# One 256-column step for the scores of the first 128 queries in the attention of a decoder block, its halves added by VectorE ahead of the sigmoid

## The chip, the cores and the metric

One core of a Trainium2 chip runs the whole program once. The metric is the device time in microseconds (us) of one execution, with the median of a few runs as the kernel's time. A profiled execution gives, beside its time, the span from its first to its last instruction and a record of each instruction on each engine.

## The reference, cut to what matters

One decoder layer on 512 tokens of width 1024, in float32: a norm, one input projection, two token mixers side by side (a chunkwise matrix memory with 8 heads, and stick-breaking attention with 8 heads), gates, an output projection, a norm, and a squared-ReLU MLP. The change lies in the scores of the attention:

```
def stick_breaking(q, k, v):
    ...
    for blk in range(S // QBLK):                       # QBLK = 128 queries
        t0, t1 = blk * QBLK, (blk + 1) * QBLK
        z = jnp.einsum('bqhd,bshd->bhqs', q[:, t0:t1], k[:, :t1]) * scale
        ...
        log_keep = jnp.where(strict, jax.nn.log_sigmoid(-z), 0.0)
        suffix = lax.cumsum(log_keep, axis=3, reverse=True) - log_keep
        A = jnp.where(strict, jnp.exp(jax.nn.log_sigmoid(z) + suffix), 0.0)
        outs.append(jnp.einsum('bhqs,bshd->bqhd', A, v[:, :t1]))
```

So query block 0 (the first 128 queries) sees 128 keys, block 1 sees 256, block 2 384 and block 3 512. The other mixer matters only because its second half of heads is worked on right after the first four attention heads: its queries and keys (`q_a`, `k_a`) go through a causal convolution of four taps and a SiLU first.

## The kernel before, in words

**Two parts per number.** Most products are made from float32 values split in two: a high part in the matmul's format (a cast on ScalarE, ACT) and the rest (value minus high part, on VectorE, DVE). `mm3` then issues three matmuls on TensorE (PE): high by high, high by low, low by high, all added up in PSUM. A weight block of 256 rows by 512 columns is loaded by `stage` into `raw_...`, split into `whi_...` (L114, ACT) and `wlo_...` (L115, DVE), and there are four buffers for each of the two, so that the fifth block's cast waits until PE has used the first. PSUM has eight banks of 512 columns: four for projections (`pp_...`), four for everything else.

**Order.** `ORDER` lists the steps by hand: `... s0 T1 s1 oa0 s2 s3 qka1 ga0 r4 r5 va1 m4 r6 m5 r7 qkb2 ...`. The steps are written out in that order, and a scheduler in the compiler then sets the order of the instructions on each engine, from that order, from stated priorities and from its own estimates of when each is ready. An engine works through its list in that fixed order. A change of one step can so move rows of other steps.

**Attention head** (`s0` to `s7`, function `sb_head`): `SEG` lists the four query blocks by j, block 3-j with n keys at column o of the head's 1280 columns of scores: j=0 has 512 columns, j=1 384, j=3 128 and j=2 256. The scores stand in three banks, `zb{h}_0` (j=0), `zb{h}_1` (j=1 and, behind it, j=3) and `zb{h}_2` (j=2, 256 columns; the other 256 are not used). For each block and each sign ACT makes a sigmoid from PSUM into `r` (of -z) and `b` (of z), L557. GpSimd (POOL) sets the upper part of each diagonal block of `b` to zero (L560), DVE makes the running products of `r` (L565) and multiplies them into `b` (L566). PE then transposes `b` in ten pieces into `zt` (L571), ACT and DVE split that into `ah` and `al` (L575, L576), and PE multiplies with the values into `po` (`mm3`).

**What comes next to heads 2 and 3.** The step `qka1` takes the projected q and k of the second four heads of the matrix memory (`xc10` to `xc13`): four taps on DVE into `cy10` to `cy13` (L399, then three rounds of L402), a sigmoid on ACT back into `xc` (L404), their product (L406), then the split into `qh1`, `ql1` and `kk1` (ACT L415 and L419, DVE L416, L418 and L420). `ga0` is a gate projection (`pp_ga`, the sigmoids `g_ga` on ACT L600, a multiply on DVE L605), `va1` the projection of the values (`pp_va`, split into `va1` by L180 and L181). `decay` for heads 4 to 6 makes exponentials `rb` on ACT (L442). Step `m4` is head 4 of the matrix memory: its scores `za4` (L451, L453), DVE scales them (L458), ACT and DVE split them into `ph4` (L460) and `pl4`, and PE multiplies them with the values into `pn4`. `qkb2` is the next projection (`pp_qkb`).

Of the kernel before, what the change touches and what calls it, by code (L numbers as in the profile page):

```python
# [10 lines left out]
AF = mybir.ActivationFunctionType  # L11
# [5 lines left out]
P = 128  # L17
# [8 lines left out]
SEG = ((0, 0, 512), (1, 512, 384), (3, 896, 128), (2, 1024, 256))  # L26
OFF = {j: o for j, o, _ in SEG}
# [5 lines left out]
HT = 256  # L33
# [30 lines left out]
def block_kernel(ctx: ExitStack, tc: tile.TileContext, x, norm_mix_g, w_in, b_if, b_gate, conv_w, mlstm_norm_g,  # L64
                 sb_q_norm_g, sb_k_norm_g, w_out, norm_mlp_g, w_up, w_down, out):
    nc = tc.nc
    act, dve, pool, pe = nc.scalar, nc.vector, nc.gpsimd, nc.tensor
# [10 lines left out]
    def f5(name):  # L78
        return ah_.tile([P, LIN], F32, tag="f5", name=name, bufs=3)

    def bank(name):
        return ps_a.tile([P, S], F32, tag="pa", name=name)

    def half_square(name):

        b = [bank(f"{name}{i}") for i in range(3)]
        return [(b[0], 0, 512), (b[1], 512, 512), (b[2], 1024, 256)]

    def part(banks, o, n):
        b, c, _ = banks[o // S]  # L90
        return b[:, o - c:o - c + n]

    def r5(name):
        return ah_.tile([P, LIN], F32R, tag="r5", name=name, bufs=4)

    def t2(tag, bufs, name):
        return at.tile([P, S], F32, tag=tag, name=name, bufs=bufs)
# [20 lines left out]
    def mm3(o, ah, al, bh, bl, start, stop, **kw):  # L118
        pe.matmul(o, ah, bh, start=start, stop=False, **kw)  # L119
        pe.matmul(o, ah, bl, start=False, stop=False, **kw)  # L120
        pe.matmul(o, al, bh, start=False, stop=stop, **kw)  # L121
# [425 lines left out]
    def sb_head(h, q, k, rq, v):  # L547

        z = half_square(f"zb{h}_")
        for j, o, n in SEG:  # L550
            il = slice((3 - j) * P, (4 - j) * P)
            mm3(part(z, o, n), q[:, 0, il], q[:, 1, il], k[:, 0, :n], k[:, 1, :n], j != 3, True,
                skip_group_check=True)
        b, r = f5(f"b{h}"), f5(f"r{h}")
        for j, o, n in SEG:
            for w, d in ((1, r), (0, b)):
                act.activation(d[:, o:o + n], part(z, o, n), AF.Sigmoid, scale=rq[:, w, 3 - j, h % 2:h % 2 + 1])  # L557
        for j, o, n in SEG:
            d = slice(o + n - P, o + n)
            pool.affine_select(out=b[:, d], in_=b[:, d], pattern=[[-1, P]], compare_op=ALU.is_gt, fill=0.0, base=0,  # L560
                               channel_multiplier=1)

        for j, o, n in SEG:
            kr = r[:, o:o + n][:, ::-1]
            dve.tensor_tensor_scan(kr, kr, msk[:, S - n:][:, ::-1], 1.0, ALU.mult, ALU.max)  # L565
        dve.tensor_mul(b[:, :LIN - 1], b[:, :LIN - 1], r[:, 1:LIN])  # L566
        zt = half_square(f"zt{h}_")
        for j, o, n in SEG:
            for i in range(j, 4):
                oi = OFF[3 - i] + P * j  # L570
                pe.transpose(part(zt, o + P * (i - j), P), b[:, oi:oi + P], ident)  # L571
        ah, al = r5(f"ah{h}"), r5(f"al{h}")
        for zz, c, n in zt:
            e = slice(c, c + n)
            act.copy(ah[:, e], zz[:, :n])  # L575
            dve.tensor_sub(al[:, e], zz[:, :n], ah[:, e].bitcast(F32))  # L576
        po = bank(f"po{h}")
        c = slice((h % 4) * P, (h % 4 + 1) * P)
        for j, o, n in sorted(SEG):
            mm3(po[:, j * P:], v[j][:, 0, c], v[j][:, 1, c], ah[:, o:o + n], al[:, o:o + n], j == 0, j == 3,  # L580
                skip_group_check=True)
        yb = t2("sy", 8, f"yb{h}")
        act.copy(yb, po)
        return yb
# [74 lines left out]
    def step(n):  # L659
        kind, i = n[:-1], int(n[-1])  # L660
        if n == "qkb1":
            load_pool[:] = [(wp, "raw", 2), (at, "raw", 1), (wp, "raw", 2)]
        if kind == "qka":
            got[n] = qka(i)
        elif kind == "r":
            got[n] = decay(i, got["qka1"][3] if i > 3 else got["qka0"][4])
        elif kind == "m":
            got[n] = mlstm_head(i, got[f"qka{i // 4}"], (v0, v1)[i // 4], got[f"r{i}"])
        elif kind == "n":
            mlstm_norm(i, [got[f"m{h}"] for h in range(i, i + 4)])  # L670
        elif kind == "va":
            v_chunk("va1", C_VA + 512, v1)
        elif kind == "vb":
            v_chunk(n, C_VB + 512 * i, vb[i])
        elif kind == "qkb":
            got[n] = qkb(i)
        elif kind == "T":
            got[n] = pair_T(got[f"qkb{i}"], i)
        elif kind == "s":
            yb[i] = sb_head(i, *got[f"T{i // 2}"][i % 2], vb[i // 4])  # L680
        elif kind == "oa":
            a_gate(i, "oa", C_OA, None)
        elif kind == "ga":
            a_gate(i, "ga", C_GA, 8)
        else:
            b_gate_(i, yb[4 * i:4 * i + 4])
# [286 lines left out]
```

## Time and profile before

| | us |
|---|---|
| time, median of 3 runs | 819.48 |
| lowest and highest of the 3 | 818.83, 820.11 |
| the profiled execution's own time | 818.37 |
| its span | 816.6 |

The profiled execution lies 1.1 us (0.14%) under the median, and 1.8 us of its time lie around its span. TensorE's granted clock was 1.00 throughout. A row of the timeline reads: start, duration, engine, line, operation, output<-inputs, sizes, count, and in brackets the idle time before it and who ended that. A matmul's end is modelled and matmuls overlap, so the spacing of their starts says what one costs. "PEld" are the loads of the stationary operand, which overlap matmuls.

### The profile page before, as it was taken

How to read it: one execution, taken by the hardware profiler on the slowest of the kernel's cores; microseconds unless marked ns; L12 is line 12 of the kernel's file. 1: busy time of each engine (PE TensorE's matmuls, PEld its weight loads, DVE VectorE, ACT ScalarE, POOL GpSimd, SP SyncE). 2: the span in 40 equal slices, each digit the busy share in tenths (PEclk: the TensorE clock that was granted, in tenths of full speed). 3: DMA queues.
4: the chain of work that ended last, by engine and by line, in shares of the span. 5: the costliest groups of instructions: out<-in, count | busy, mean ns of one | idle time of the engine just before them, and what ended most of it. 6: DMA issues, size and time to landing. Idle time of an engine off the chain costs nothing.

```text
span 816.6 us, 11540 instructions
## 1 busy us (share of the span) xinstructions
PE 806.2 (99%) x4380; PEld 692.7 (85%) x4380; DVE 599.1 (73%) x826; ACT 457.3 (56%) x681; POOL 165.0 (20%) x216
## 2 busy tenths in 40 slices
PE   8999999999999999999999999999999999999998
PEld 6878887888888887888888888999999999999876
DVE  6669967584598486756653659898689868978994
ACT  6429756654557468545552437576466545655541
POOL 3015323111221140010120101223302421232220
PEclk9999999999999999999999999999999999999999
DMA  9354542353423423522257406987977995999963
GB/s 233 91 156 143 120 80 64 82 104 84 152 91 94 118 65 67 142 66 77 78 188 270 109 4 155 208 178 160 204 226 158 182 224 166 188 200 188 228 125 100
DMA packets 64408, 113.65 MB, mean 139 GB/s; under 512 B 5793, under 2 KB 18129, under 8 KB 64354
## 3 DMA queue, kind: packets, MB, share of 16 engines
q1 hardware_dynamic: 44770, 71.43, 31.3%
q0 software_dynamic: 19584, 41.50, 26.6%
q8 instruction: 34, 0.56, 0.3%
q14 instruction: 20, 0.16, 0.1%
HBM read 110.74 MB, written 2.17 MB: 138 GB/s over the span
## 4 chain that ended last, share of the span: by engine, by line
PE 93%; DVE 3%; ACT 1%; DMA 1%; issue 1%; SPq 0%; ACTq 0%; DVEq 0%
PE pp_qkb L121 4%; PE pp_qkb L119 4%; PE pp_qkb L120 4%; PE pp_yup L119 3%; PE pp_yup L120 3%; PE pp_yup L121 3%; PE ydn L119 2%; PE ydn L120 2%; PE ydn L121 2%; PE pp_qka L119 2%; PE pp_zup L120 2%; PE pp_va L120 2%; PE pp_zup L121 2%; PE pp_qka L120 2%; PE pp_xup L120 2%; PE pp_zup L119 2%
## 5 line engine op out<-in xcount | busy, mean ns | idle before, releaser
L560 POOL TENSOR_SCALAR_AFFINE_SELECT b<-b 128x128 f32<-128x128 f32 x32 | 19.0, 609 | 161.3 <-ACT b L557 161.3
L120 PE MATMUL pp_qkb<-wlo_qkb,hT 128*128 128x512 f32 x128 | 50.2, 392 | 0.0
L121 PE MATMUL pp_qkb<-whi_qkb,hT 128*128 128x512 f32 x128 | 50.0, 393 | 0.0
L119 PE MATMUL pp_qkb<-whi_qkb,hT 128*128 128x512 f32 x128 | 49.3, 391 | 0.0
L766 POOL DMA_DIRECT2D raw_Xup<-in_w_up_dram x24 | 28.9, 1243 | 84.8 <-DVE wlo_p5up L727 37.6
L766 POOL DMA_DIRECT2D raw_Xdn<-in_w_down_dram x18 | 21.6, 1214 | 102.6 <-DVE wlo_p5dn L727 36.1
L565 DVE TENSOR_TENSOR_SCAN r<-r,msk 128x512 f32<-128x512 f32 (+3 forms) x32 | 25.1, 832 | 13.8 <-ACT r L557 13.8
L115 DVE TENSOR_TENSOR wlo_qkb<-raw_qkb,whi_qkb 128x1024 fp32r<-128x1024 f32 x16 | 21.7, 1365 | 14.1 <-ACT whi_qkb L114 14.0
L119 PEld LDWEIGHTS pp_qkb<-whi_qkb,hT 128*128 128x128 f32 x128 | 24.1, 188 | 5.1
L121 PEld LDWEIGHTS pp_qkb<-whi_qkb,hT 128*128 128x128 f32 x128 | 24.0, 188 | 5.1
L120 PEld LDWEIGHTS pp_qkb<-wlo_qkb,hT 128*128 128x128 f32 x128 | 24.1, 188 | 4.7
L897 ACT ACTIVATE uq<-uq 128x512 f32<-128x512 f32 x32 | 20.0, 630 | 12.2 <-DVE uq L896 12.0
L120 PE MATMUL pp_va<-wlo_va,hT 128*128 128x512 f32 x64 | 24.9, 392 | 0.8 <-DVE wlo_va L292 0.8
L119 PE MATMUL pp_ga<-hT,whi_ga 128*128 128x512 f32 x64 | 25.3, 395 | 0.0
L119 PE MATMUL pp_qka<-hT,whi_qka 128*128 128x512 f32 x64 | 25.2, 396 | 0.0
L120 PE MATMUL pp_qka<-hT,whi_qka 128*128 128x512 f32 x64 | 25.2, 393 | 0.0
L121 PE MATMUL pp_oa<-hT,wlo_oa 128*128 128x512 f32 x64 | 25.1, 392 | 0.0
L120 PE MATMUL pp_wo<-wlo_wo,y 128*128 128x512 f32 x64 | 25.1, 392 | 0.0
L120 PE MATMUL pp_ga<-hT,whi_ga 128*128 128x512 f32 x64 | 25.1, 392 | 0.0
L120 PE MATMUL pp_oa<-hT,whi_oa 128*128 128x512 f32 x64 | 25.1, 392 | 0.0
L119 PE MATMUL pp_vb<-whi_vb,hT 128*128 128x512 f32 x64 | 25.0, 391 | 0.0
L120 PE MATMUL pp_gb<-hT,whi_gb 128*128 128x512 f32 x64 | 25.0, 391 | 0.0
(571 smaller groups left out, 2955.2 us busy)
## 6 DMA issues: line engine op xcount, KB each, us to landing
raw_Xup<-in_w_up_dram POOLq DMA_DIRECT2D x24, 512.0 KB, 7.2
raw_Xdn<-in_w_down_dram POOLq DMA_DIRECT2D x18, 512.0 KB, 6.9
raw_qkb<-in_w_in_dram SPq DMA_DIRECT2D x32, 256.0 KB, 3.9
rb<-rows POOLq DMA_DIRECT2D x8, 640.0 KB, 5.4
raw_va<-in_w_in_dram SPq DMA_DIRECT2D x8, 512.0 KB, 5.2
raw_qka<-in_w_in_dram SPq DMA_DIRECT2D x16, 256.0 KB, 6.6
raw_vb<-in_w_in_dram SPq DMA_DIRECT2D x8, 512.0 KB, 4.5
raw_oa<-in_w_in_dram SPq DMA_DIRECT2D x8, 512.0 KB, 4.2
```

The source lines that it names most:

```text
L115: dve.tensor_sub(lo, raw, hi.bitcast(F32))
L119: pe.matmul(o, ah, bh, start=start, stop=False, **kw)
L120: pe.matmul(o, ah, bl, start=False, stop=False, **kw)
L121: pe.matmul(o, al, bh, start=False, stop=stop, **kw)
L560: pool.affine_select(out=b[:, d], in_=b[:, d], pattern=[[-1, P]], compare_op=ALU.is_gt, fill=0.0, base=0, channel_multiplier=1)
L565: dve.tensor_tensor_scan(kr, kr, msk[:, S - n:][:, ::-1], 1.0, ALU.mult, ALU.max)
L766: pool.dma_start(out=buf[b, j], in_=src(more, j), accum_op=ALU.add)
L897: act.activation(h(r, c), h(r, c), AF.Square)
```

## The change

Per head, the three matmuls of query block 0 (128 columns each) go. In their place, behind the three of j=2, stand one matmul of 256 columns (L555: the high part of the queries by both parts of the keys, into the unused half of `zb{h}_2`) and one of 128 columns (L556: the low part of the queries by the high part of the keys, added to the first half). ACT then copies the first half into `b` (L558), DVE adds the second half to it (L559), and the two sigmoids of j=3 read `b` in place of PSUM.

```diff
-        for j, o, n in SEG:
+        for j, o, n in sorted(SEG)[:3]:
             il = slice((3 - j) * P, (4 - j) * P)
-            mm3(part(z, o, n), q[:, 0, il], q[:, 1, il], k[:, 0, :n], k[:, 1, :n], j != 3, True,
-                skip_group_check=True)
+            mm3(part(z, o, n), q[:, 0, il], q[:, 1, il], k[:, 0, :n], k[:, 1, :n], True, True, skip_group_check=True)
+
+        x = z[2][0][:, HT:].rearrange("p (w n) -> p w n", w=2)
+        pe.matmul(x, q[:, 0, :P], k[:, :, :P], start=False, stop=False, skip_group_check=True)
+        pe.matmul(x[:, 0, :], q[:, 1, :P], k[:, 0, :P], start=False, stop=True, skip_group_check=True)
         b, r = f5(f"b{h}"), f5(f"r{h}")
+        act.copy(b[:, OFF[3]:OFF[3] + P], x[:, 0, :])
+        dve.tensor_add(b[:, OFF[3]:OFF[3] + P], x[:, 1, :], b[:, OFF[3]:OFF[3] + P])
         for j, o, n in SEG:
             for w, d in ((1, r), (0, b)):
-                act.activation(d[:, o:o + n], part(z, o, n), AF.Sigmoid, scale=rq[:, w, 3 - j, h % 2:h % 2 + 1])
+                act.activation(d[:, o:o + n], part(z, o, n) if j != 3 else b[:, o:o + n], AF.Sigmoid,
+                               scale=rq[:, w, 3 - j, h % 2:h % 2 + 1])
```

Lines behind the edit have numbers that are six higher than before (the sigmoid L557 is L562, the transposes L571 are L577). The scheduler's order moves as well, most of all between head 1 and head 5 of the attention.

Place 1, PE, the scores of head 2; before:

```order
L119 MATMUL zb2_1_1775<-kT2_1549,qT2_1541 128x384
L120 MATMUL zb2_1_1775<-kT2_1549,qT2_1541 128x384
L121 MATMUL zb2_1_1775<-kT2_1549,qT2_1541 128x384
L119 MATMUL zb2_1_1775<-kT2_1549,qT2_1541 128x128
L120 MATMUL zb2_1_1775<-kT2_1549,qT2_1541 128x128
L121 MATMUL zb2_1_1775<-kT2_1549,qT2_1541 128x128
L119 MATMUL zb2_2_1776<-kT2_1549,qT2_1541 128x256
L120 MATMUL zb2_2_1776<-kT2_1549,qT2_1541 128x256
L121 MATMUL zb2_2_1776<-kT2_1549,qT2_1541 128x256
```

and with the change:

```order
L119 MATMUL zb2_1_1777<-kT2_1550,qT2_1542 128x384
L120 MATMUL zb2_1_1777<-kT2_1550,qT2_1542 128x384
L121 MATMUL zb2_1_1777<-kT2_1550,qT2_1542 128x384
L119 MATMUL zb2_2_1778<-kT2_1550,qT2_1542 128x256
L120 MATMUL zb2_2_1778<-kT2_1550,qT2_1542 128x256
L121 MATMUL zb2_2_1778<-kT2_1550,qT2_1542 128x256
L555 MATMUL zb2_2_1778<-kT2_1550,qT2_1542 128x256
L556 MATMUL zb2_2_1778<-kT2_1550,qT2_1542 128x128
```

Three matmuls of 128 columns became one of 256 and one of 128, behind j=2.

Place 2, PE, from the last projection matmul of `va1` to the scores of head 4 of the matrix memory and on; before:

```order
L121 MATMUL pp_va13_2283<-whi_va13_2376,hT1_151 128x512
L451 MATMUL za4_0_2416<-qh10_2078,kk10_2079 128x512
L453 MATMUL za4_0_2416<-ql10_2080,kk10_2079 128x512
...
L451 MATMUL za4_2_2418<-qh10_2078,kk10_2079 128x256
L453 MATMUL za4_2_2418<-ql10_2080,kk10_2079 128x256
L119 MATMUL pp_qkb20_2530<-whi_qkb20_2537,hT0_150 128x512
L120 MATMUL pp_qkb20_2530<-wlo_qkb20_2538,hT0_150 128x512
L121 MATMUL pp_qkb20_2530<-whi_qkb20_2537,hT1_151 128x512
```

and with the change:

```order
L121 MATMUL pp_va13_2287<-whi_va13_2380,hT1_151 128x512
L451 MATMUL za4_0_2420<-qh10_2082,kk10_2083 128x512
L453 MATMUL za4_0_2420<-ql10_2084,kk10_2083 128x512
...
L451 MATMUL za4_2_2422<-qh10_2082,kk10_2083 128x256
L453 MATMUL za4_2_2422<-ql10_2084,kk10_2083 128x256
L119 MATMUL pn4_2445<-ph4_2431,va10_2408 128x512
L451 MATMUL za5_0_2477<-qh10_2082,kk10_2083 128x512
```

Before, 27 matmuls of the projection `qkb2` stand between `za4` and the first of `pn4`; now `pn4`, which reads `ph4`, follows `za4` at once, and `qkb2` comes after it and after `za5`.

Place 3, DVE and ACT, around the convolution of `qka1`, behind attention head 3. DVE before:

```order
L576 TENSOR_TENSOR al3_1892<-zt3_0_1878,ah3_1891 128x512
L576 TENSOR_TENSOR al3_1892<-zt3_1_1879,ah3_1891 128x512
L576 TENSOR_TENSOR al3_1892<-zt3_2_1880,ah3_1891 128x256
L115 TENSOR_TENSOR wlo_va11_2317<-raw_va11_2314,whi_va11_2316 128x1024
L399 TENSOR_SCALAR cy10_2050<-xc10_2042,vec_128 128x512
```

and with the change (`g_ga00` to `g_ga02` are gates of `ga0`):

```order
L582 TENSOR_TENSOR al3_1896<-zt3_2_1884,ah3_1895 128x256
L611 TENSOR_TENSOR yq0_480<-yq0_480,g_ga00_2236 128x512
L611 TENSOR_TENSOR yq0_480<-yq0_480,g_ga01_2239 128x512
L611 TENSOR_TENSOR yq0_480<-yq0_480,g_ga02_2242 128x512
L115 TENSOR_TENSOR wlo_va13_2381<-raw_va13_2378,whi_va13_2380 128x1024
L399 TENSOR_SCALAR cy10_2054<-xc10_2046,vec_128 128x512
```

ACT with the change, from the last gate to the exponentials of `decay` (before, the four L404 stand together, right behind `g_ga03`):

```order
L606 ACTIVATE g_ga03_2245<-pp_ga03_2115,vec_128 128x512
L589 COPY yb3_1916<-po3_1903 128x512
L114 CAST whi_qkb20_2541<-raw_qkb20_2538 128x1024
L404 ACTIVATE xc10_2046<-cy10_2054 128x512
L114 CAST whi_qkb21_2572<-raw_qkb21_2569 128x1024
L404 ACTIVATE xc11_2047<-cy11_2055 128x512
L404 ACTIVATE xc12_2048<-cy12_2056 128x512
L404 ACTIVATE xc13_2049<-cy13_2057 128x512
L442 ACT_TABLE_LOAD
L442 ACTIVATE rb4_2248<-rb4_2248,cc_413 128x512
```

Three gate multiplies and a weight split now stand ahead of the taps on DVE, and two weight casts among the sigmoids on ACT. The transposes `zt3` of head 3, too, stand later on PE: between them and `za4` there are 159 matmuls before (150 of 512 columns, three each of 384, 256 and 128) and 122 with the change (113 of 512, the same others).

## The prediction, made before the changed kernel ran

> **What bounds the kernel.** I read the page first, then who waits on TensorE (PE), then busy time by stage, then the timelines of the engines around the attention heads. The page's busy time and its chain that ended last:
>
> ```profile
> PE 806.2 (99%) x4380; PEld 692.7 (85%) x4380; DVE 599.1 (73%) x826; ACT 457.3 (56%) x681; POOL 165.0 (20%) x216
> PE 93%; DVE 3%; ACT 1%; DMA 1%; issue 1%; SPq 0%; ACTq 0%; DVEq 0%
> ```
>
> PE is the bound. The two longest waits on PE in the view of who waited for whom:
>
> ```profile
> PE pw L230 <- DVE warm L189: 1.5, 1, 1.5
> PE ydn L120 <- DVE wlo_p6dn L727: 1.1, 1, 1.1
> ```
>
> No wait is longer than 1.5 us, the first is the program's start, and the second lies in the MLP. Busy time in two of the stages that hold attention heads (PE is the second and third number, then the loads, DVE, ACT, POOL, granted clock):
>
> ```profile
> 200.00:257.00 57.00, 57.00 (x273) 47.92 (x272) 40.30 (x57) 36.62 (x61) 10.64 (x23) 1.00 0.35 109
> 275.00:440.00 165.00, 165.00 (x803) 137.68 (x802) 102.16 (x146) 88.96 (x144) 21.76 (x28) 1.00 0.41 120
> ```
>
> PE is never idle there. So two things count: what the edit takes from PE's own work, and whether the new order makes PE wait where it never did.
>
> **What the edit takes from PE.** The scores of head 0 in the timeline:
>
> ```profile
> 148.32 0.22 PE L119 MATMUL zb<-kT,qT 128*128 128x128 f32 x1
> 148.32 0.19 PEld L120 LDWEIGHTS zb<-kT,qT 128*128 128x128 f32 x1
> 148.38 0.27 PE L120 MATMUL zb<-kT,qT 128*128 128x128 f32 x1
> 148.43 0.19 PEld L121 LDWEIGHTS zb<-kT,qT 128*128 128x128 f32 x1
> 148.49 0.27 PE L121 MATMUL zb<-kT,qT 128*128 128x128 f32 x1
> 148.60 0.33 PE L119 MATMUL zb<-kT,qT 128*128 128x256 f32 x1
> 148.77 0.28 PE L120 MATMUL zb<-kT,qT 128*128 128x256 f32 x1
> 148.89 0.28 PE L121 MATMUL zb<-kT,qT 128*128 128x256 f32 x1
> ```
>
> Matmuls of 128 columns start 0.11 us apart (148.38, 148.49, 148.60), as their weight loads do (148.32, 148.43); those of 256 columns start 0.12 apart (148.77, 148.89). Both cost about one weight load, so three steps become two: 0.11 us less per head, 0.9 in eight. The ends: spacing 0.06 for a 128-column matmul that hides behind a longer one (148.32 to 148.38) gives 0.05 per head, 0.4 in all; the recorded durations (0.22+0.27+0.27 against 0.28+0.27) give 0.21 per head, 1.7 in all. I take 0.9, since the spacing is what the next matmul sees.
>
> A rule speaks against even that. The Trainium skill, "TensorE: Matmul & The Clock Gate", section "Back-to-back issue gap", puts an isolated warm matmul at N/2.4 + 2.5 ns; worked out from it, an estimate, three of 128 columns are 167 ns and one of 256 plus one of 128 are 165, so the saving would be nothing and the sum 0.9 us higher. The 0.11 us spacing disagrees with its 56 ns for 128 columns.
>
> **What it adds on ACT and DVE.** The copy is nearest to a 128x128 sigmoid, the add to a 128x128 multiply by a column:
>
> ```profile
> 151.75 0.38 ACT L557 ACTIVATE r<-zb,rq 128x128 f32<-128x128 f32 x1
> 152.00 0.39 ACT L557 ACTIVATE b<-zb,rq 128x128 f32<-128x128 f32 x1
> L530 DVE TENSOR_SCALAR nat<-nat,ssq x32: 274/279/1036, 99.4 to 336.9; 128x128 f32<-128x128 f32 x32
> ```
>
> That is 0.25 us (start to start) by 8 on ACT, and 0.28 by 8 on DVE: 2 us each, between nothing and 3 (8 by the full 0.38). I cost them at nothing directly: PE's own work covers them in these stages, with DVE at 40 of 57 us and ACT at 37. If that cover is gone they count in full in the head's chain, which is also longer because j=3 waits for the copy and the add. No DMA and no queue entry is added.
>
> **What the new order does.** The scheduler has answered the longer chain by putting the transposes later, those of head 3 by several us, and this pushes the convolution of `qka1`. Its chain ends in `kk10` and `ph4`, which PE needs for `za4` and `pn4`. PE now (the two `pp_va` rows are 75 matmuls apart, so 0.2267 us each):
>
> ```profile
> 220.44 1.25 PE L571 MATMUL zt<-ident,b 128*128 128x128 f32 x10
> 239.65 0.39 PE L119 MATMUL pp_va<-whi_va,hT 128*128 128x512 f32 x1
> 256.65 0.39 PE L121 MATMUL pp_va<-whi_va,hT 128*128 128x512 f32 x1
> 256.88 0.39 PE L451 MATMUL za<-qh,kk 128*128 128x512 f32 x1
> 258.14 0.40 PE L119 MATMUL pp_qkb<-whi_qkb,hT 128*128 128x512 f32 x1
> 264.29 0.40 PE L119 MATMUL pn<-ph,va 128*128 128x512 f32 x1
> ```
>
> Let Z be the end of `zt3` on PE, 221.5 before (ten starts of 0.109 from 220.44). `za4` starts at Z+35.4 and `pn4` at Z+42.8. With the change 37 matmuls fewer stand between `zt3` and `za4`: 37 by 0.2267 is 8.4, so PE is ready for `za4` at Z+27.0, and for `pn4`, which now follows at once, 1.26 later (258.14 less 256.88), at Z+28.2: 14.6 us earlier after `zt3` than before. Now the other side, DVE and then ACT:
>
> ```profile
> 221.70 1.62 DVE L576 TENSOR_TENSOR al<-zt,ah 128x512 fp32r<-128x512 f32 x3 [3.28 <-ACT ah L575]
> 224.55 1.67 DVE L399 TENSOR_SCALAR cy<-xc,vec 128x512 f32<-128x512 f32 x4
> 226.13 2.83 DVE L402 SCALAR_TENSOR_TENSOR cy<-xc,vec,cy 128x511 f32<-128x511 f32 x4
> 234.51 1.28 DVE L605 TENSOR_TENSOR yq<-yq,g_ga 128x512 f32<-128x512 f32 x2
> 237.04 1.21 DVE L115 TENSOR_TENSOR wlo_va<-raw_va,whi_va 128x1024 fp32r<-128x1024 f32 x1
> 249.08 1.40 DVE L420 TENSOR_TENSOR kk<-cy,kk 64x512 fp32r<-64x512 f32 x2
> ```
>
> ```profile
> 235.09 1.05 ACT L114 CAST whi_va<-raw_va 128x1024 fp32r<-128x1024 f32 x1 [0.44 <-PE pp_ga L120]
> 236.05 1.26 ACT L600 ACTIVATE g_ga<-pp_ga,vec 128x512 f32<-128x512 f32 x2
> 238.94 1.29 ACT L404 ACTIVATE xc<-cy 128x512 f32<-128x512 f32 x2 [0.60 <-DVE cy L402]
> 240.25 1.28 ACT L442 ACT_TABLE_LOAD   x1
> 241.55 5.55 ACT L442 ACTIVATE rb<-rb,cc 128x512 f32<-128x512 f32 x12
> 247.01 1.25 ACT L415 CAST qh<-cy 64x512 fp32r<-64x512 f32 x2
> 248.28 1.26 ACT L419 CAST kk<-cy 64x512 fp32r<-64x512 f32 x2
> 255.04 1.95 ACT L180 CAST va<-pp_va 128x512 fp32r<-128x512 f32 x3
> 258.86 0.63 ACT L460 CAST ph<-rb 128x512 fp32r<-128x512 f32 x1 [0.20 <-DVE rb L458]
> ```
>
> Before, `kk10` is complete at 250.5, Z+29.0, which `za4` at Z+35.4 does not feel but at Z+27.0 would: even with the old chain PE comes up 2 us short. The new chain, in us after Z:
>
> - DVE: `al3` ends at 1.8 (223.3 before). Then three gate multiplies of 0.6, paced by two buffers for the gates on ACT: 4.1. ACT casts `whi_va13` by 4.4, DVE its lower part (1.15) by 5.6. Taps: four L399 (1.6), a gate multiply (0.6), nine L402 at 0.67 (6.0): `cy10` is done at 13.8 (the old order had its first tap at Z+3.0).
> - ACT: `xc10` 0.6, to 14.5. The cast `whi_qkb21` stands next and needs the buffer of `whi_va11`, which PE reads last 74 matmuls after `zt3`, at 16.1 (35.4 less 85 by 0.2267); such waits are seen in the row at 235.09. With it 17.1; three L404 at 0.58 18.9; table load 1.3, 20.2; ten of the twelve L442 rows (4.9 of 5.5) 25.0; `qh10` 1.3, the other two L442 0.6, `kk10` 1.3: 28.2. DVE adds its half of `kk10` by 29.0: `za4` starts there, not at 27.0.
> - ACT goes on in its order: `qh11` 1.3, a weight cast 0.95, `kk11` 1.3, three `va1` casts at 0.5, a weight cast, the fourth `va1`, and `ph4` 0.6: 35.2.
>
> PE, ready at 28.2, starts `pn4` at 35.3: 7.1 us lost, 2.0 of them ahead of `za4`. Behind it waits all of `qkb2`, which could have run. DVE has `va10` out of its projection bank at Z+35.1, so the bank does not hold `qkb2` any longer. Ends: 5.8 if the buffer wait is not met (the taps would then set 17.6 for `xc13`, 1.3 sooner), 8 if DVE and ACT each lose half a us more to the waits between them.
>
> I find no gain of this kind: in 140 to 440 PE had nothing to lose, and behind `gb1` the order on PE is the old one, so the loss is not given back. Sum: 818.4 of the profiled execution, less 0.9, plus 7.1, is 824.6; the median lies 1.1 above that execution, so 825.7.
>
> **Rivals.**
>
> *The wait also costs clock (18%).* The first matmuls of the program and later ones:
>
> ```profile
> 1.54 3.47 PE L230 MATMUL pw<-warm 128*128 128x512 f32 x8 [1.54 <-DVE warm L189]
> 8.34 1.41 PE L230 MATMUL pw<-warm 128*128 128x512 f32 x5
> ```
>
> Eight of 512 columns take 3.5 us from the start, about 0.43 each, and 0.25 later: a start from idle costs 8 by 0.2, some 1.5 us. The idle time at `pn4` would be 5 us in one piece, longer than any here. If it counts as a start from idle, 827.2. The Trainium skill, on the page named above, section "Part 1: The HAM clock gate", says that about 3.4 us of idling, in a window that runs free, halve the clock; by that rule a gap of 5 us is caught about every second time, and no gap in this trace is long enough to test it.
>
> *A partial wait (13%).* If the scores' chain runs ahead on ACT where I let it wait, 2 to 5 us are lost: 820.5 to 823.6. For it: my sum has 30 pieces. Against it: `kk10` alone is 2 us short.
>
> *No wait, the edit does what it says (9%).* Then 818.6, no change. It needs `ph4` 7 us sooner than the fixed lists of ACT and DVE allow.
>
> *Faster (3%).* No wait, and a matmul worth its recorded duration: 1.7 us less, 817.8, and with any more faster than the limit. It decides once a 128-column matmul costs over 0.2 us; the spacing of 0.11 speaks against it.
>
> *More waits (4%).* A head's transposes could wait too, above all head 1, where the sigmoids' table load now comes behind the copy: 829 and more.
>
> **How the numbers follow.** The likeliest case, 53%, runs from 824.4 (5.8 lost) to 826.6 (8 lost). Down to 821.0 and up to 828.6 the range takes in the clock and most of the partial wait. A difference of 0.2%, 1.6 us, is about what a measurement of this kernel can tell from none: 817.8 to 821.1. Faster 0.04, same 0.12, slower 0.84.
>
> **What the changed profile would show.** Right: PE with a wait of about 2 us at `za` for DVE's `kk` and of about 5 at `pn` for ACT's `ph`, both new; L399 of the second half some 13 us later than 224.5; ACT idle ahead of `whi_qkb` for PE; the first matmul behind `za4` being `pn`; all heads' scores 0.11 shorter; from `qkb2` on everything 6 us later. Wrong: PE full through 257 to 275, or `cy` starting right behind `al3`, or the loss standing at another head's `zt`.

## The result and the profile after

The changed kernel takes 829.97 us (median; 828.88 to 831.51) against 819.63 us: 1.0137 times as long, 95% interval 1.0125 to 1.0149. The forecast was 825.7 us with a range of 821.0 to 828.6, so slower was right and the size was not. In the medians below, one execution of the kernel before (4615 us) and one of e10 (1632 us) are left out as slow.

The page after, its busy time and its chain that ended last:

```profile
PE 807.3 (98%) x4372; PEld 693.3 (84%) x4372; DVE 601.8 (73%) x834; ACT 456.2 (55%) x687; POOL 170.5 (21%) x216
PE 90%; ACT 4%; DVE 4%; issue 1%; DMA 0%; SPq 0%; ACTq 0%; DVEq 0%
```

The span is 826.8 us, 10.2 more than before, and PE does almost the same work in it. So the time went into waits of PE, and into matmuls at a lower clock. The three new waits in the view of who waited for whom:

```profile
PE pn L119 <- ACT ph L460: 5.5, 1, 5.5
PE pp_qka L119 <- ACT g_oa L604: 2.6, 1, 2.6
PE za L451 <- DVE kk L420: 1.3, 1, 1.3
```

The prediction named `pn` and `za`; it did not name `pp_qka`. Busy time by stage, columns as in the prediction (PE, loads, DVE, ACT, POOL, granted clock). Before, in the two stages in question:

```profile
140.00:200.00 60.00, 60.00 (x299) 49.73 (x298) 40.70 (x53) 35.89 (x62) 7.51 (x12) 1.00 0.38 80
257.00:275.00 18.00, 18.00 (x93) 15.44 (x92) 12.60 (x17) 8.37 (x13) 8.15 (x13) 1.00 0.45 124
```

and after:

```profile
140.00:200.00 60.00, 57.42 (x287) 47.45 (x286) 36.97 (x52) 33.44 (x57) 6.36 (x8) 1.00 0.40 89
200.00:257.00 57.00, 57.00 (x273) 47.88 (x272) 38.79 (x53) 31.55 (x56) 16.50 (x27) 1.00 0.35 109
257.00:275.00 18.00, 11.21 (x46) 9.17 (x45) 16.74 (x23) 11.87 (x20) 5.69 (x7) 0.81 0.23 58
```

PE was full in all three before. Now 2.6 us are missing in the first and 6.8 in the third, and in the third the clock is 0.81 on the mean. The rows of the third stage, in the timeline of PE:

```profile
230.77 1.25 PE L577 MATMUL zt<-ident,b 128*128 128x128 f32 x10
260.24 0.47 PE L451 MATMUL za<-qh,kk 128*128 128x512 f32 x1 [1.30 <-DVE kk L420]
267.24 0.80 PE L119 MATMUL pn<-ph,va 128*128 128x512 f32 x1 [5.49 <-ACT ph L460]
267.84 0.63 PE L451 MATMUL za<-qh,kk 128*128 128x512 f32 x1
270.19 0.63 PE L119 MATMUL pp_qkb<-whi_qkb,hT 128*128 128x512 f32 x1
270.94 0.39 PE L121 MATMUL pp_qkb<-whi_qkb,hT 128*128 128x512 f32 x1
```

From 267.24 to 270.94 the starts lie about twice as far apart: `pn` takes 0.60 for 0.23, the eight of `za5` 2.35 where `za4` took 1.26 before (256.88 to 258.14), two of `qkb2` 0.75 for 0.45. Together 1.75 us lost.

The wait in the first stage comes behind head 1's scores. Before (ACT, then PE):

```profile
173.05 1.28 ACT L557 ACT_TABLE_LOAD   x1
174.35 0.69 ACT L557 ACTIVATE r<-zb,rq 128x512 f32<-128x512 f32 x1
177.64 1.14 ACT L598 ACTIVATE g_oa<-pp_oa 128x512 f32<-128x512 f32 x2
172.85 0.39 PE L119 MATMUL zb<-kT,qT 128*128 128x512 f32 x1
174.76 0.39 PE L119 MATMUL pp_oa<-hT,whi_oa 128*128 128x512 f32 x1
177.96 0.39 PE L121 MATMUL pp_oa<-hT,wlo_oa 128*128 128x512 f32 x1
178.34 0.50 PE L119 MATMUL pp_qka<-hT,whi_qka 128*128 128x512 f32 x1
```

and after:

```profile
175.01 0.27 ACT L558 COPY b<-zb 128x128 f32<-128x128 f32 x1 [2.22 <-PE zb L556]
175.30 1.28 ACT L562 ACT_TABLE_LOAD   x1
176.59 0.69 ACT L562 ACTIVATE r<-zb,rq 128x512 f32<-128x512 f32 x1
179.68 1.11 ACT L604 ACTIVATE g_oa<-pp_oa 128x512 f32<-128x512 f32 x2
173.06 0.39 PE L119 MATMUL zb<-kT,qT 128*128 128x512 f32 x1
174.82 0.45 PE L119 MATMUL pp_oa<-hT,whi_oa 128*128 128x512 f32 x1
175.10 0.40 PE L120 MATMUL pp_oa<-hT,whi_oa 128*128 128x512 f32 x1
180.36 0.50 PE L119 MATMUL pp_qka<-hT,whi_qka 128*128 128x512 f32 x1 [2.58 <-ACT g_oa L604]
```

Before, ACT loaded the sigmoids' table while PE still made the scores. Now the copy stands first in ACT's list, it waits for the last matmul of the scores (174.75 to 174.82), and the table load comes behind it. The sigmoids start 2.24 us later, the gates' sigmoid `g_oa` 2.04 later, and PE needs the bank that it empties. There was no slack to lose: before, `pp_qka` already started 0.38 behind the matmul ahead of it where 0.23 is usual, and three matmuls of `pp_oa` fewer stand ahead of it now.

The same rows give what the edit saves on PE: from the first score to the first matmul behind them 1.91 us before, 1.76 after, of which the next spacing (0.28 for 0.23) takes back 0.05: 0.10 us in this head, 0.8 in eight if all save the same. The sum: 1.30 + 5.49 + 2.43 (2.58 less the 0.15 that was there) + 1.75 less 0.8 is 10.2, and the spans differ by 10.2.

### The profile page after: what moved, and what is told of

The parts are those of the page before. It is cut to its first block, busy times and chain, and to the rows that moved or that the text cites. A ratio compares the mean times of both kernels' runs of the same rounds, so it can differ in the third digit from the quotient of the medians.

```text
span 826.8 us, 11546 instructions
## 1 busy us (share of the span) xinstructions
PE 807.3 (98%) x4372; PEld 693.3 (84%) x4372; DVE 601.8 (73%) x834; ACT 456.2 (55%) x687; POOL 170.5 (21%) x216
## 4 chain that ended last, share of the span: by engine, by line
PE 90%; ACT 4%; DVE 4%; issue 1%; DMA 0%; SPq 0%; ACTq 0%; DVEq 0%
PE pp_qkb L119 4%; PE pp_qkb L121 4%; PE pp_qkb L120 4%; PE pp_yup L119 3%; PE pp_yup L120 3%; PE pp_yup L121 3%; PE ydn L120 2%; PE ydn L119 2%; PE ydn L121 2%; PE pp_qka L119 2%; PE pp_zup L120 2%; PE pp_zup L121 2%; PE pp_qka L120 2%; PE pp_gb L119 2%; PE pp_zup L119 2%; PE pp_qka L121 2%
## 5 line engine op out<-in xcount | busy, mean ns | idle before, releaser
L566 POOL TENSOR_SCALAR_AFFINE_SELECT b<-b 128x128 f32<-128x128 f32 x32 | 21.1, 669 | 175.8 <-ACT b L562 137.0
L114 ACT CAST whi_qkb<-raw_qkb 128x1024 fp32r<-128x1024 f32 x16 | 16.8, 1052 | 21.0 <-PE pp_qkb L121 7.7
L571 DVE TENSOR_TENSOR_SCAN r<-r,msk 128x512 f32<-128x512 f32 (+3 forms) x32 | 24.7, 826 | 4.6 <-ACT r L562 4.6
L121 PE MATMUL pp_ga<-hT,wlo_ga 128*128 128x512 f32 x64 | 25.2, 393 | 0.0
L120 PE MATMUL pp_ga<-hT,whi_ga 128*128 128x512 f32 x64 | 25.2, 393 | 0.0
L121 PE MATMUL pp_gb<-hT,wlo_gb 128*128 128x512 f32 x64 | 25.1, 392 | 0.0
L120 PE MATMUL pp_vb<-wlo_vb,hT 128*128 128x512 f32 x64 | 25.0, 391 | 0.0
```

Of the source, the lines that this page charges most:

```text
L114: act.copy(hi, raw)
```

## The experiments

The kernel before took 818.91 us in the runs e1 to e4, 818.33 in e5 to e8 and 818.78 in e9 and e10.

**e1: the 256-column matmul cut in two.**

```diff
-pe.matmul(x, q[:, 0, :P], k[:, :, :P], ...)
+pe.matmul(x[:, 0, :], q[:, 0, :P], k[:, 0, :P], ...)
+pe.matmul(x[:, 1, :], q[:, 0, :P], k[:, 1, :P], ...)
```

> The 256-column matmul of each head is cut into two of 128 columns (high by high into the first half, high by low into the second); copy and add stay, and the order of the engines around heads 0 to 5 stays that of the change. It prices the one thing that the change takes from TensorE. Theory A (the loss is three waits on TensorE, at the first qka1 matmul 2.6, za4 1.3 and pn4 5.5 us, plus a halved clock after pn4, all made by the order; the 256-column step saves 0.1 us per head): the same waits within 0.5 us, 0.05 to 0.11 us more per head, so 830.4 to 830.9 against 830.0 of the change. Rival B (the 256-column step itself is what is slow): back towards 820 to 824, with the waits at za4 and pn4 gone or halved.

832.47 us (ratio 1.0169, 1.0155 to 1.0183). The waits are the same to 0.1 us, so the 256-column step isn't what is slow. My number was 1.6 us too low: the clock of all four executions was 0.994 (0.996 in three of four of the change), and the profile has a second stretch at half clock, near the end of the MLP. So the total can't price the 128-column matmul; the starts in the trace do.

**e2: no copy and no add.**

```diff
-act.copy(b[...], x[:, 0, :])
-dve.tensor_add(b[...], x[:, 1, :], b[...])
-... part(z, o, n) if j != 3 else b[:, o:o + n] ...
+... part(z, o, n) if j != 3 else x[:, 0, :] ...
```

> The copy and the add are left out; both sigmoids of query block 0 read the first half in PSUM directly, so the product of the high part of the queries with the low part of the keys is missing from the scores of that block. The 256-column step stays. The order on TensorE around head 4 of the matrix memory is that of the kernel before (27 qkb2 matmuls between za4 and pn4). Theory A: no wait over 0.5 us at qka1, za4 or pn4, clock 1.00, and the 0.1 us per head is all that is left: 818.5 to 819.1 against 819.6 of the kernel before. Rival B (the 256-column step is slow): 825 or more. Rival C (the copy and the add as work on ScalarE and VectorE, 4 us in all, cost about half the loss): 824 to 826.

818.70 us (0.9999, 0.9990 to 1.0008). None of the three waits is over 0.3 us. The whole loss hangs on the copy and the add, as work or by the order that they bring (e9 parts the two); the step on PE costs nothing, and its saving can't be told from none.

**e3: copy, add and their sigmoids behind the six others.**

```diff
-for j, o, n in SEG:
+for j, o, n in sorted(SEG):
+    if j == 3:
+        act.copy(...); dve.tensor_add(...)
```

> The copy, the add and the two sigmoids of query block 0 stand behind the six sigmoids of the other three blocks instead of ahead of and among them. The taps of qka1 come as late as with the change; pn4 stands 20 rows behind za4, not directly behind it. Theory A: the table load of head 1 runs beside the scores again, so the wait of 2.6 us at the first qka1 matmul falls to under 0.5; at za4 a wait of 1 to 3.5 us for kk10, at pn4 0 to 2 us since 4.3 us of qkb2 stand ahead of it; no idle stretch over 4 us, so the clock stays at 1.00: 820 to 824, likeliest 822. Rival C (copy and add as work cost the time wherever they stand): 828 to 831.

828.44 us (1.0121, 1.0107 to 1.0135): a miss by 6. Who waited on PE:

```profile
PE za L451 <- DVE kk L420: 3.9, 1, 3.9
PE pp_qkb L119 <- DVE va L181: 2.3, 1, 2.3
PE pp_qka L119 <- ACT g_oa L605: 0.4, 1, 0.4
```

Head 1 came out as said (2.6 to 0.4), so what I called the price of the copy's place is right, and rival C's "wherever they stand" is not. But the 20 rows ahead of `pn4` did not help: it waits no more, and PE stops elsewhere. PE came to `za4` 3.9 us too soon, and behind it `qkb2` needed a bank that `va1` still held. I had reckoned with neither the bank nor the clock, at half from 260.4 to 270.8.

**e4: useless matmuls in the gap.**

```diff
+for t in range(20 if h == 4 else 0):
+    pe.matmul(pn, qh[pr][:, i, :P], qh[pr][:, i, :], start=True, stop=True, ...)
 for j, o, n in sorted(SEG):
     mm3(pn[:, j * P:], ...)
```

> The change, with 20 useless matmuls of 512 columns (4.5 us) between za4 and the first matmul of pn4, written into pn4's bank and overwritten by it; the output is unchanged, and the order around it is that of the change. It takes the idle stretch from TensorE without making ph4 any sooner. Theory A with the clock (a halved clock for 6.7 us costs 1.75 us of the loss): pn4 starts as late as with the change, the granted clock is 1.00 throughout, 1.5 to 2 us faster than the change in its better executions: 827 to 828.3. Rival D (the reading of the clock has no price, matmuls behind the gap are slow for another reason): 829.5 to 831, with matmuls of 0.4 us spacing still behind pn4.

The third stage and rows of PE in it:

```profile
257.00:275.00 18.00, 15.96 (x74) 12.91 (x73) 16.56 (x23) 11.82 (x21) 5.92 (x6) 1.00 0.23 56
```

```profile
261.78 4.74 PE L470 MATMUL pn<-qh 128*128 128x512 f32 x20
266.36 0.39 PE L451 MATMUL za<-qh,kk 128*128 128x512 f32 x1
267.61 0.39 PE L119 MATMUL pn<-ph,va 128*128 128x512 f32 x1
268.74 0.50 PE L119 MATMUL pp_qkb<-whi_qkb,hT 128*128 128x512 f32 x1 [0.73 <-DVE va L181]
269.07 0.39 PE L120 MATMUL pp_qkb<-wlo_qkb,hT 128*128 128x512 f32 x1
```

`pn` comes no sooner, but the clock is 1.00 and the matmuls behind the gap are at their usual spacing. So rival D's slow matmuls behind `pn` are not there. The order is not quite that of the change: the eight matmuls of `za5` stand ahead of `pn` here, and `qkb2` waits 0.73 us for a bank. So the span, 824.9 and 1.9 us under that of the change, fits the 1.75 that the starts gave but is not the clock's price alone. The other three executions stood at 0.997 to 0.998 and took 828.5 to 829.3 (median of all 828.70): their lower clock says that it fell somewhere else, and their records don't show where; e10 bears on it.

**e5: the change in heads 4 to 7 only.**

```diff
-yb[i] = sb_head(i, ...)
+yb[i] = (sb_head if i > 3 else sb_old)(i, ...)     # sb_old: as before
```

> The change in heads 4 to 7 only; heads 0 to 3 are as before, and so is the order of the engines up to the first scores of head 4. Theory A (the loss is waits of TensorE at three places around heads 1 to 3, and the clock behind them): none of the three waits, clock 1.00, four heads' saving of 0.1 us: 818.2 to 819.0 where the kernel before takes 818.9 to 819.6. Rival C (copy, add and the longer chain cost some 1.3 us in each head): 823 to 825.

817.59 us (0.9992, 0.9983 to 1.0000), the fastest version here, though hardly to be told from before. PE is full again in the third stage:

```profile
257.00:275.00 18.00, 18.00 (x93) 15.43 (x92) 12.68 (x16) 8.26 (x13) 8.15 (x13) 1.00 0.41 123
```

Four heads cost nothing, so it isn't a price per head; the loss belongs to heads 0 to 3.

**e6: the change in head 1 only** (as e5, with `i == 1`).

> The change in head 1 only. The copy stands ahead of the table load of head 1 as with the change. The taps of qka1 stand two rows behind al3, as before, but pn4 follows za4 directly, as with the change. It parts what the last runs left together: pn4's place and the late taps. Theory A2 (e3 shows: late taps alone cost the time around za4; pn4's place alone costs little, since ph4 follows za4 by 2.6 us when kk10 is early): 2.6 at the first qka1 matmul, under 0.5 at za4, 1 to 2.5 at pn4: 822 to 824. Theory A1 (pn4's place is the main cause, as the prediction had it): 5 us or more at pn4, with a halved clock behind it: 826 to 828.

828.56 us (1.0123, 1.0106 to 1.0140).

```profile
PE pn L119 <- ACT ph L460: 5.2, 1, 5.2
PE pp_qka L119 <- ACT g_oa L643: 1.9, 1, 1.9
```

My theory A2 falls: one head, with the taps two rows behind `al3`, makes the wait at `pn4`. But the run does not part the two things that it was made to part. In time the taps were not early: they stand behind a `wlo_va` that waits for PE, and start at 232.32, 3.9 us behind `al3` and 7.8 us later than before the change. So late taps with 20 rows ahead of `pn4` (e3) stop PE for 6.2 us, late taps with `pn4` directly behind `za4` for 5.2 (e6) and 6.8 (the change): PE stops at whatever first needs the end of one chain. What `pn4`'s place would cost with early taps, no run shows.

**e7: buffers of their own for the heads' outputs.**

```diff
-y = [t2("sy", 8, f"cy{i}{o}") for o in range(4)]     (and s likewise)
+y = [t2("sy", 4, f"cy{i}{o}") for o in range(4)]
-yb = t2("sy", 8, f"yb{h}")
+yb = t2("yb", 4, f"yb{h}")
```

> The change, with the eight buffers that the taps' results (cy), the sums s and the heads' outputs (yb) share cut into four for yb and four for the others. No arithmetic changes. Then the taps no longer have to come behind yb3, the output of head 3, and the scheduler puts them 52 rows ahead of al3; 24 rows stand between za4 and pn4. Theory A2 (late taps, because cy10 may take its buffer only behind yb3, are what makes the waits at za4 and pn4): these two fall to under 0.5 us, the one at the first qka1 matmul stays at 2.6, clock 1.00 or one short fall: 820.3 to 822 where before takes 818.9. Rival A1 or C: 825 or more.

828.03 us (1.0118, 1.0102 to 1.0133). `za` and `pn` wait no more, as A2 said, but the time is 6 us above its range, where the rivals had it. PE is held up elsewhere:

```profile
PE pp_va L119 <- ACT g_ga L606: 3.9, 1, 3.9
PE pp_qka L119 <- ACT g_oa L604: 2.6, 1, 2.6
```

These waits are 6.5 us, and the clock is at half for 3.4 us around the end of the one at `pp_qka` and for 6.8 around the end of the other. So the shared buffers are why the taps came late. That `cy10` could take one only behind `yb3`, head 3's output, is my reading of the scheduler's order and not shown: in time, the taps before the change start at 224.55, ahead of the copy into `yb3` at 228.66. With the tie cut, the freed work lands among head 3's sigmoids.

**e8: e7 and e3 together.**

> As the run before, and with the copy, the add and the two sigmoids of query block 0 behind the six others, so that the table load of head 1 has nothing ahead of it. Theory A2: no wait of TensorE over 0.5 us that the kernel before doesn't have, clock 1.00, and the 0.1 us per head is left: 818.0 to 818.7 where before takes 818.9; not to be told from no change by more than a hair. Rival: other waits come up where the taps now run beside head 3's scans (its transposes later): 820 to 823.

822.71 us (1.0054, 1.0041 to 1.0067); its rival was right. One wait is left, and the timeline of ACT shows its cause:

```profile
PE pp_va L119 <- ACT g_ga L607: 2.6, 1, 2.6
```

```profile
227.40 1.28 ACT L442 ACT_TABLE_LOAD   x1
228.70 1.92 ACT L442 ACTIVATE rb<-rb,cc 128x512 f32<-128x512 f32 x4
230.64 1.28 ACT L563 ACT_TABLE_LOAD   x1
233.48 1.24 ACT L607 ACTIVATE g_ga<-pp_ga,vec 128x512 f32<-128x512 f32 x2
```

Four exponentials among the sigmoids cost 1.92 us and two table loads, 4.5 in all, ahead of the gate for which PE waits. The clock is at half for 3.4 us around the end of that wait.

**e9: e8, the exponentials held behind the gates.**

```diff
-got[n] = decay(i, got["qka1"][3] if i > 3 else got["qka0"][4])
+got[n] = decay(i, last["ga0"] if i > 3 else got["qka0"][4])     # the last sigmoid of ga0
```

> As e8, with the exponentials of heads 4 to 7 of the matrix memory held behind the last sigmoid of ga0 in place of the last sigmoid of qka1. In e8 ScalarE loads a table for four of them in the middle of head 3's sigmoids and loads the sigmoids' table back (2 by 1.28 us, with 1.92 of exponentials), and TensorE waits 2.6 us for the gate behind them. Theory A2 (the loss is nothing but waits that the order makes; the edit itself costs nothing): the wait at the first va1 matmul falls under 0.5 us, no other comes, clock 1.00, all eight heads changed: 817.6 to 818.5 where before takes 818.3 to 818.9. Rival (every order of the changed kernel pays somewhere, since its chain on ScalarE and VectorE is longer): a new wait of 1.5 us or more at za4, pn4 or head 3's products, 820 or more.

818.74 us (0.9997, 0.9989 to 1.0006), 0.2 above the range that I gave. All eight heads are changed, no new wait is over 0.7 us, and the loss is gone; the rival falls. It is no gain either.

**e10: e9 with the copy ahead of all sigmoids, as in the change.**

> As e9, but with the copy and the add ahead of all sigmoids, as in the change. The only difference to e9 in the program is that place, so that the difference between the two is the price of the copy ahead of head 1's table load. Theory A: one wait of 2.5 to 2.7 us at the first qka1 matmul, and in most executions one window of halved clock of 3.4 us behind it (1 to 1.7 us more): 2.5 to 4.3 us over e9, so 820.3 to 822.5. Rival (the wait at qka1 of the changed kernel came from the order behind it, not from the copy's place): within 1 us of e9.

822.07 us (1.0033, 1.0020 to 1.0045), 3.3 over e9. Its one new wait on PE is that of the change again, 2.6 us at `pp_qka` for `g_oa`. The profiled execution had no fall of the clock there and took 820.46; five others stood at 0.997 to 0.998 and took 821.9 to 822.3. So the place of these lines (the copy and the add, and with them the two sigmoids of query block 0, ahead of those of j=2 again) costs 2.6 us of waiting. Executions with the lower clock took 1.4 to 1.9 us more.

## Why the prediction was wrong, step by step

**Scores on PE: right.** 0.11 us per head forecast, 0.10 by the starts. The formula for isolated matmuls of the Trainium skill, "TensorE: Matmul & The Clock Gate", section "Back-to-back issue gap", by which nothing would be saved, is not borne out by the starts. The same section says that it under-counts small matmuls, since it leaves out the weight loads. The totals (e2, e5, e9) can't decide between 0 and 0.9.

**The chain to `ph4`: right, nearly to the tenth.** With Z the end of `zt3`, 231.9 (ten starts from 230.77), `za4` started at Z+28.4 (forecast 29.0) and `pn4` at Z+35.4 (35.3); the two waits are 6.8 us (7.1). The signs that I gave for it are there, among them taps that start at 237.55, 13.0 us later. The rows it went through:

```profile
239.73 6.16 DVE L402 SCALAR_TENSOR_TENSOR cy<-xc,vec,cy 128x511 f32<-128x511 f32 x9
248.10 1.06 ACT L114 CAST whi_qkb<-raw_qkb 128x1024 fp32r<-128x1024 f32 x1 [1.54 <-PE pp_va L121]
259.41 1.40 DVE L420 TENSOR_TENSOR kk<-cy,kk 64x512 fp32r<-64x512 f32 x2 [0.57 <-ACT kk L419]
266.57 1.35 ACT L460 CAST ph<-rb 128x512 fp32r<-128x512 f32 x2
```

The first nine taps end at Z+14.0 (13.8), and the cast that waits for PE's buffer starts at Z+16.2 (16.1). What I did not see is that the late taps would have been enough, with 20 rows of `qkb2` ahead of `pn4` too (e3). My reason that DVE had the bank free and `qkb2` "could have run" does not hold: DVE has the first tile of `va1` out of its bank at 268.4, behind the start of `pn4`, and in e3, where `qkb2` does stand there, PE waits for that bank.

**The copy and the add: the step that failed.** "I cost them at nothing directly: PE's own work covers them" took the cover from mean busy times (DVE 40 of 57 us, ACT 37). In head 1 there was none: ACT emptied a bank of `pp_oa` just when PE needed it. It is not the copy's 0.27 us that costs, but that ACT waits there with the table load and everything else behind it. The table load behind the copy stood among the rivals, with 4%, and with the wrong waiter, the transposes. It cost 2.4 us, which the sum put at nothing; e3 and e10 show it, since the wait goes and comes with the place of these lines.

**The clock: in the rivals at 18%, and it came.** 1.5 us were priced by the program's first matmuls, 1.75 measured. By the Trainium skill's rule, from the same page's "Part 1: The HAM clock gate" (idling of some 3.4 us, in a window that runs free), a gap of 5 us would be caught about every second time; all four executions of the change, and all four of e1, stand at 0.996 or less, where the kernel before stands at 0.998 to 1.000.

**The sum.** The likeliest case was without either, and the range's upper end lay about where one came alone. Both came: 824.6 of the profiled execution, plus 2.4 and 1.75, is 828.8; it took 828.9. I had set rivals that can come together side by side as if each excluded the others.

## What to carry to other kernels

An instruction put into an engine's list is priced first by what it waits for and what stands behind it there, and only then by its length: ahead of a table load that used to run beside other work, a copy of 0.27 us cost 2.4. Where a bound engine has no idle time, look for the rows at which it starts exactly when its operand or bank comes free, since there the slack is nothing whatever the busy shares say. If order lists shift, a wait that is removed may come back at the next tie (e3, e7, e8), so take apart the ties (shared buffers, banks, table loads) one by one, and add up risks that can come together.

## What the runs showed of the hardware

The stretches at half clock last 3.4, 6.8 or 10.2 us in these profiles, and some of them took less idling than I thought. Three windows with what follows each (PE's busy time, granted clock), of the change, e7 and e1:

```profile
260.54:263.95 3.41, 1.22 (x8) 1.00 0.00 0
263.95:270.77 6.82, 3.53 (x11) 0.50 0.31 79
```

```profile
176.74:180.15 3.41, 1.12 (x5) 1.00 0.49 120
180.15:183.56 3.41, 3.12 (x7) 0.50 0.00 0
```

```profile
802.62:806.03 3.41, 1.87 (x8) 1.00 0.34 101
806.03:809.44 3.41, 3.41 (x10) 0.50 1.01 157
```

In these three the 3.4 us ahead of the fall were not idle: PE was busy for 1.1 to 1.9 us of them. (In e3 and e6 they were, ahead of `za4` and `pn4`.) In e1 the waits of that window were 1.1 and 0.4 us. The Trainium skill, "TensorE: Matmul & The Clock Gate", section "Part 1: The HAM clock gate", has the length of the window (3413 ns), which the traces bear out, and at least one idle window before the fall, which they don't.

The same wait of 2.58 us at `pp_qka` brought no fall in the profile of the change and one in that of e7. Behind it the first matmuls start 0.33 and 0.23 us apart in the change (180.36, 180.69, 180.92) and 0.60 and 0.43 apart in e7 (180.44, 181.04, 181.47): that is what the clock costs, with the same gap ahead. Within one profile, any two changes of the clock lie a whole multiple of 3.413 us apart: in e7 the second fall comes 58.03 us, 17 of them, behind the first. Counted back so from the fall at 263.95, a window of the change ends at 178.62. It splits the gap (177.78 to 180.36) into 0.84 and 1.74 us, while in e7 2.3 us of it lie in the one window that ends at 180.15. So where the window lies seems to decide, and it would explain why e10's executions differ by up to 1.9 us. It is not the whole rule: the second of these windows of the change, with PE busy for 1.7 us, brought no fall, and the one of e1, with 1.9, did. That stays open.
